# A hand-ordered attention kernel: short dummy matmuls in its head, V cast two pairs at a time, Newton's roots in PSUM, and new instruction orders

## The chip, the cores and the metric

The kernel runs on one core of a Trainium2 chip. A core has five engines with a queue each: TensorE (PE in the profile; PEld is its loading of weights), VectorE (DVE), ScalarE (ACT), GpSimd (POOL) and SyncE (SP), which here only issues DMAs. Each works through its own list in order and waits on semaphores for the others. The metric is the device time of one execution in microseconds (us), lower is better. Three runs of the kernel before gave 189.88, 192.01 and 192.94 us; their median is 192.01.

## The reference

```python
batch, heads, seq, dim = 8, 12, 512, 64        # Q, K, V float32, tau = 0.1
Q_norm = Q / (np.linalg.norm(Q, axis=-1, keepdims=True) + 1e-10)
K_norm = K / (np.linalg.norm(K, axis=-1, keepdims=True) + 1e-10)
scores = np.einsum('bhqd,bhkd->bhqk', Q_norm, K_norm) / tau
weights = np.exp(scores - np.max(scores, axis=-1, keepdims=True))
weights = weights / (np.sum(weights, axis=-1, keepdims=True) + 1e-10)
return np.einsum('bhqk,bhkd->bhqd', weights, V).astype(np.float32)
```

It is attention with cosine similarity: the rows of Q and K are brought to length one, and so the scores lie between -10 and 10 and their exponentials need no maximum taken off.

## The kernel before, in words

The 96 heads are worked in 48 pairs (`s` in the code), each head of a pair with 512 rows of 64 numbers, laid out as 128 partitions by 4 rows. For a pair:

- SP loads Q, K (`LD`, L312 and L315) and V (`LV`, L318) into rings of 17 and 9 buffers.
- POOL squares Q and K (`SQ`, L341; L335 for the first pairs, a part of which ACT does, L333).
- The sums of squares (`RED`) come in two ways: DVE adds up 64 columns itself (L369), or PE first adds eight groups of columns with an identity matrix (`SSQ`, L358) and DVE adds the remaining eight (L365). In the first four pairs both Q and K go over PE.
- The inverse roots (`NEW`) are made by DVE for a whole group of one to four pairs: a first guess by integer arithmetic on the bits (L403), then two Newton steps of three instructions each (L394, L395, L399). For pairs 0 and 1 ACT makes them by logarithm and exponential (L256 and L258, L383 and L386).
- Q and K are scaled by them and cast to bf16 (`SCL`, L427; Q on DVE, K mostly on POOL). PE transposes them (`TR`, L433) into PSUM, DVE copies them out (`EVA`, L441).
- PE makes the scores in four chunks of 128 keys by two heads by 512 queries (`SCO`, L532) in two alternating PSUM buffers of two banks each. ACT takes the exponential of a chunk in one instruction of 128x1024 (`EXP`, L548). One chunk in all, chunk 3 of pair 43 (the table `OFF`), goes through a polynomial on DVE and POOL instead (`poly`).
- POOL casts V to bf16, beside a column of ones (`VC`, L553). PE multiplies (`PV`, L565), DVE divides by the column sums (`RCP` L576, `NRM` L578), and SP stores the pair (`ST`, L582).

Pair 0 goes through a head of its own (`head0`): it is loaded, squared, scaled, transposed and scored by single heads (L521), and its exponentials are 8 of 128x512 (L524), with K's inverse norm as their scale. Before it PE runs eight matmuls on zeros (`warm`, L191) and one more dummy (L194). A dummy writes into the second of the two PSUM banks that PV uses. The last pair's end is cut into pieces (`last`).

Nothing sets the order at run time. `ORDER` holds, for each engine, the list of all its operations by number, with negative numbers for dummy matmuls of so many columns; the waits are worked out from the needs that `P.add` is given. An engine that waits holds up everything behind it.

## Time and profile before

| | |
|---|---|
| Runs | 189.88, 192.01, 192.94 us (median 192.01) |
| Span of the profiled execution | 190.9 us |
| Its own time outside the profile | not given; the span is all that the page has |
| ACT busy | 182.7 us, 96% of the span |
| PE, DVE, POOL busy | 175.9, 170.2, 161.8 us |
| Large exponentials | 186, 171.3 us busy, 0.6 us idle before them |
| First large exponential starts | 15.18 us |
| Last instruction of ACT ends | 188.8 us |

The page gives busy times, a picture of the span in 40 slices, the chain of work that ended last, and groups of instructions with the idle time before them. In rows of groups "x186 | 171.3, 1113 | 0.6" means 186 instructions, 171.3 us busy together, 1113 ns each, and 0.6 us in which their engine had been idle just before them. Instructions of one engine overlap a little at their ends, so the mean is longer than the distance from one to the next. A row of the chain has its start, its length, and the engine, tile and line.

### The profile page before, as it was taken

Reading aid. Unit: us, or ns where it says so; the run is one execution under the profiler, and the core shown is the slowest. Engines: PE = TensorE matmul, PEld = TensorE weight load, DVE = VectorE, ACT = ScalarE, POOL = GpSimd, SP = SyncE. Lnnn points to the kernel's source line nnn. Section 1 sums busy time; section 2 is a strip of 40 time slices with the busy share of each in tenths; the row PEclk is TensorE's granted clock in tenths of the full one; section 3 lists DMA queues with packets and bytes.
Section 4 is the critical chain, followed back from the end, with each engine's and each line's share of the span. In section 5 each row is a group of like instructions: output and inputs, shape, how many; then the busy total and the mean of one; then the engine's idle time right before and its main releaser. Section 6 shows DMA issues by size and latency. Waiting matters only on the chain.

```text
span 190.9 us, 6650 instructions
## 1 busy us (share of the span) xinstructions
PE 175.9 (92%) x2705; PEld 109.4 (57%) x2705; DVE 170.2 (89%) x552; ACT 182.7 (96%) x215; POOL 161.8 (85%) x150
## 2 busy tenths in 40 slices
PE   7699699999999999999999999999999899897973
PEld 2355266666656666666566666556656565464642
DVE  2668999999999999999997998999999999988642
ACT  5678999999999999999999999999999999999994
POOL 5397898999999999999999999999999994793000
PEclk9958999999999999999999999999999999999998
DMA  5999999997999599999979999999950414000565
GB/s 162 344 348 349 350 348 372 365 297 250 268 351 337 169 260 320 357 366 369 380 277 272 351 377 364 354 379 384 365 194 5 165 58 165 3 0 3 193 197 165
DMA packets 52446, 50.76 MB, mean 266 GB/s; under 512 B 3136, under 2 KB 52416, under 8 KB 52416
## 3 DMA queue, kind: packets, MB, share of 16 engines
q1 hardware_dynamic: 51984, 50.02, 79.7%
q8 instruction: 21, 0.34, 0.8%
q10 hardware_dynamic: 432, 0.33, 0.5%
q14 instruction: 9, 0.07, 0.1%
HBM read 37.75 MB, written 12.58 MB: 264 GB/s over the span
## 4 chain that ended last, share of the span: by engine, by line
ACT 89%; PE 4%; DMA 3%; DVE 1%; issue 0%; SPq 0%
ACT et L548 88%; DMA qk<-in_Q_dram 3%; PE ops L358 2%; PE scps L521 1%; PE tps L433 1%; DVE qn L427 1%; PE scps L532 0%; SPq L312 0%; ACT et L543 0%; ACT sq L333 0%; ACT ob L608 0%; PE tps L270 0%; DVE qn L261 0%; DVE ob L612 0%; PE ops L593 0%
## 5 line engine op out<-in xcount | busy, mean ns | idle before, releaser
L548 ACT ACTIVATE et<-scps 128x1024 bf16<-128x1024 f32 x186 | 171.3, 1113 | 0.6 <-PE scps L532 0.4
L341 POOL TENSOR_TENSOR sq<-qk 128x1024 bf16<-128x1024 f32 x44 | 83.1, 1896 | 0.1
L532 PE MATMUL scps<-qt 64*128 64x512 bf16 x374 | 73.3, 387 | 6.3 <-ACT et L548 3.3
L565 PE MATMUL ops<-vb,et 128*128 128x65 bf16 x1504 | 72.8, 195 | 1.7 <-DVE ob L578 1.0
L565 PEld LDWEIGHTS ops<-vb,et 128*128 128x128 bf16 x1504 | 55.3, 98 | 30.9 <-issue 18.3
L427 POOL TENSOR_TENSOR qn<-qk,rk 128x512 bf16<-128x512 f32 x38 | 39.5, 1045 | 5.9 <-PE scps L532 3.7
L578 DVE TENSOR_TENSOR ob<-ops,rd 128x256 f32<-128x256 f32 x94 | 38.8, 418 | 0.7
L427 DVE TENSOR_TENSOR qn<-qk,nps 128x512 bf16<-128x512 f32 x56 | 37.2, 677 | 0.7 <-ACT nps L386 0.6
L433 PE MATMUL tps<-ident,qn 128*128 128x128 bf16 x376 | 34.3, 222 | 0.9 <-POOL qn L427 0.3
L441 DVE COPY qt<-tps 128x1024 bf16<-128x1024 bf16 x47 | 32.1, 682 | 0.4 <-PE tps L433 0.4
L532 PEld LDWEIGHTS scps<-qt 64*128 64x128 bf16 x374 | 18.2, 92 | 23.5 <-ACT et L548 9.6
L369 DVE TENSOR_REDUCE nps<-sq 128x8 f32<-128x512 bf16 x46 | 30.8, 682 | 0.8 <-POOL sq L341 0.7
L553 POOL TENSOR_SCALAR vb<-vf 128x512 bf16<-128x512 f32 x48 | 29.7, 630 | 0.1
L433 PEld LDWEIGHTS tps<-ident,qn 128*128 128x128 bf16 x376 | 21.9, 99 | 12.0 <-issue 5.4
L576 DVE RECIPROCAL rd<-ops 128x4 f32<-128x4 f32 x94 | 16.1, 174 | 6.6 <-PE ops L565 5.9
L358 PE MATMUL ops<-sq,ident 128*128 128x64 bf16 x384 | 20.0, 199 | 0.1
L358 PEld LDWEIGHTS ops<-sq,ident 128*128 128x128 bf16 x384 | 15.2, 101 | 4.3 <-issue 2.5
L365 DVE TENSOR_REDUCE nps<-ops 128x8 f32<-128x64 f32 x46 | 10.0, 218 | 0.9 <-PE ops L358 0.7
L394 DVE TENSOR_TENSOR nps<-nps,ys 128x32 f32<-128x32 f32 (+2 forms) x34 | 7.0, 207 | 0.4
L395 DVE SCALAR_TENSOR_TENSOR nps<-nps,ys 128x32 f32<-128x32 f32 (+2 forms) x34 | 7.0, 206 | 0.4
L335 POOL TENSOR_TENSOR sq<-qk 128x512 bf16<-128x512 f32 (+1 forms) x5 | 4.7, 956 | 3.2 <-DMA qk<-in_K_dram 2.8
L524 ACT ACTIVATE et<-scps,xs 128x512 bf16<-128x512 f32 x8 | 4.9, 682 | 0.3 <-PE scps L521 0.3
(66 smaller groups left out, 57.8 us busy)
## 6 DMA issues: line engine op xcount, KB each, us to landing
vf<-in_V_dram SPq DMA_DIRECT2D x48, 256.0 KB, 6.6
qk<-in_Q_dram SPq DMA_DIRECT2D x47, 256.0 KB, 5.5
qk<-in_K_dram SPq DMA_DIRECT2D x47, 256.0 KB, 6.3
out_dram<-ob SPq DMA_DIRECT2D x47, 256.0 KB, 5.7
qk<-in_Q_dram SPq DMA_DIRECT2D x2, 128.0 KB, 2.7
qk<-in_K_dram ACTq DMA_DIRECT2D x2, 128.0 KB, 2.8
out_dram<-ob SPq DMA_DIRECT2D x1, 128.0 KB, 1.7
out_dram<-ob SPq DMA_DIRECT2D x1, 64.0 KB, 1.6
```

Source lines behind the costliest of these rows:

```text
L341: lambda e: e.tensor_tensor(out=sqf, in0=data, in1=data, op=ALU.mult))
L358: last = e.matmul(out=o_ps[bank][:, 320:384], lhsT=ident[:, :], rhs=sq[iqs][:, 8 * w : 8 * w + 8, 8 * k : 8 * k + 8], start=(k == 0), stop ...
L369: lambda e, w=w, dst=dst: e.tensor_reduce(out=dst, in_=sq[iqs][:, 8 * w : 8 * w + 8, :], axis=AX.X, op=ALU.add))
L427: lambda e, w=w, r=r: e.tensor_tensor(out=qn[iqn][:, w].rearrange("p t h d -> p h t d"), in0=qk[iq][:, w].rearrange("p h (t d) -> p h t d" ...
L433: last = e.transpose(t_ps[:, w, t, :], qn[iqn][:, w, t].rearrange("p h d -> p (h d)"), ident[:, :])
L441: lambda e: e.tensor_copy(out=qt[iqt][:, :, :, :].rearrange("p w t x -> p (w t x)"), in_=t_ps[:, :, :, :].rearrange("p w t x -> p (w t x)")))
L532: last = e.matmul(out=sc_ps[:, 2 * b + h, :], lhsT=qt[iqt][64 * h : 64 * h + 64, 1, c, :], rhs=qt[iqt][64 * h : 64 * h + 64, 0, :, :], sta ...
L548: lambda e, c=c, b=b: e.activation(out=et[iet][:, c, :, :], in_=sc_ps[:, 2 * b : 2 * b + 2, :], func=ACT.Exp, scale=math.log(2.0) / UNIT i ...
L553: lambda e: e.tensor_scalar(out=vb[:, iq, :, :, 0:DIM].rearrange("p c h d -> p h c d"), in0=vf[iv][:, :, :].rearrange("p h (c d) -> p h c ...
L565: last = e.matmul(out=o_ps[h][:, 65 * t : 65 * t + 65], lhsT=et[iet][:, c, h, 128 * t : 128 * t + 128], rhs=vb[:, iq, c, h, :], start=(c = ...
L576: lambda e, h=h, grid=grid: e.reciprocal(out=rd[io][:, h, :], in_=grid[:, :, DIM]))
L578: lambda e, h=h, grid=grid: e.tensor_tensor(out=ob[io][:, h], in0=grid[:, :, 0:DIM], in1=rd[io][:, h, :].unsqueeze(2).to_broadcast([128, N ...
```

## The change

- **Dummies.** The eight warm-up matmuls stay. The one dummy of 256 columns gives way to fourteen of 128 columns, spread over PE's list from the first transposes to the second part of pair 0's PV.
- **Sums in one bank.** The norm sums that PE makes for pairs 1 to 3 all go through the first PV bank; before, Q's went through the first and K's through the second. Each waits for DVE's reduction of the one before.
- **V.** Its f32 buffers become one tensor with a ring of 8 pairs (9 before), its bf16 buffers get a ring of their own of 16 (17, shared with Q and K, before) and another layout. From pair 4 on POOL casts two pairs in one instruction, which waits for both loads.
- **Newton.** The sums and iterates lie in SBUF (`xs`, `ts`), the roots in PSUM (`n_ps`); before, sums and iterates were in PSUM and the guesses in SBUF. Where DVE scales some K of a group, its last step makes Q's and K's roots at once, in place of two steps; where it scales all of them, the step for POOL's copy goes too. Counted over all groups, 144 steps become 135.
- **Polynomial.** It is written in another form: three POOL steps in place of four, two DVE steps as before. A scale that was an instruction of its own (`UNIT`) moves into the constants of Newton's last step, and the exponentials of the four pairs of that group get another scale.
- **Orders.** All five lists of `ORDER` are new.

```diff
-        session[s, w] = (w, due_red(s), before[w])
-        before[w] = [("RED", s, w)]
+        session[s, w] = (0, due_red(s), before[0])
+        before[0] = [("RED", s, w)]
...
+    def news(g):
+        if g in NORM_ON_ACT:
+            return [7] if direct_r(g) else [6, 7]
+        return [*range(6), *([6] if on_pool(g) else []), 7]
+
+    def on_pool(g):
+        return [i for i in range(first[g], first[g] + sizes[g]) if i not in K_ON_DVE]
...
-        xg = n_ps[:, g % R_X, 0 : 2 * m]
-        tg = n_ps[:, g % R_X, 64 : 64 + 2 * m]
-        yg = ys[g % R_X][:, 0 : 2 * m]
+        xg, tg, yg = xs[g % R_X][:, 0 : 2 * m], ts[g % R_X][:, 0 : 2 * m], n_ps[:, g % R_X, 0 : 2 * m]
...
-                yx, yyx, up(yg, 0, 2 * m), yx, yyx, up(rq_g, 0, m), up(rk_g, m, 2 * m)]
-            if on_dve:
-                steps.append(up(tg[:, m : 2 * m], m, 2 * m))
+                1: yx, 2: yyx(1.0), 3: up(yg, 0, 2 * m, 1.0), 4: yx, 5: yyx(c_g), 6: up(rk_g, m, 2 * m, c_g),
+                7: up(yg, 0, 2 * m, c_g) if on_dve else up(rq_g, 0, m, c_g)}
...
-        steps = [("pool", "yt", mul(z, z, z)), ("pool", "ys", add(w, z, a1)), ("pool", "yt", mul(w, w, w))]
-        if form == "A":
-            steps += [("pool", "ys", add(w, w, a2)), ("dve", "yd", fused(e_, z, a3, w)), ("dve", "ym", mul(e_, e_, p2))]
+        steps = [
+            ("pool", "yt", mul(z, z, z)),
+            ("pool", "ys", lambda e: e.tensor_scalar(out=w, in0=z, scalar1=a1, scalar2=a2, op0=ALU.add, op1=ALU.mult)),
+            ("pool", "yt", mul(w, w, z)),
+            ("dve", "yd", lambda e: e.scalar_tensor_tensor(out=e_, in0=w, scalar=a3, in1=z, op0=ALU.add, op1=ALU.mult)),
+            ("dve", "ym", mul(e_, e_, p2))]
...
+        n = len(cast_with[s])
+        if s == cast_with[s][0]:
+            P.add(("VC", s), "pool", f"vc{n}" if n > 1 else "vc", T0 + 3.0 - slack(s, M_VC),
+                  [("LV", i) for i in cast_with[s]] + [key("PV", i - R_VB, h, NT - 1) for i in cast_with[s] for h in range(2)] + ["vone"],
+                  lambda e: e.tensor_scalar(
+                      out=vb[:, ivb : ivb + n, :, :, 0:DIM].rearrange("p n h c d -> p (n h c) d"),
+                      in0=vf[:, iv : iv + n].rearrange("p n h (c d) -> p (n h c) d", c=NT),
+                      scalar1=1.0, scalar2=1.0, op0=ALU.mult, op1=ALU.mult))
...
-RINGS = (17, 9, 6, 4, 4, 5, 8, 3)
+RINGS = (17, 8, 16, 6, 4, 4, 5, 8, 3)
+MOST = 64
+CAST_ALONE = 4
+CAST_TOGETHER = 2
...
     "pe": (
-        "6 24 22 -256 38 52 40 36 76 78 44 48 54 42 114 46 116 83 85 50 159 87 161 89 57 58 59 63 91 60 128 130 93 "
+        "6 24 22 -128 38 44 52 -128 36 48 -128 40 -128 76 78 -128 54 42 -128 -128 -128 -128 114 46 116 -128 -128 "
```

Three places in the orders. In them `qn` are scaled rows, `qt` transposed ones, `scps` scores, `ops` the two PV banks, `tps` the bank of transposes, `ys` or `ya` logarithms, `xs` or `xa` sums and inverse norms. PE, from the end of the warm-up to the norm sums of pair 1, before:

```order
L272 MATMUL ops<-ident,qn 64x128 x4
L272 MATMUL tps<-ident,qn 64x128 x4
L194 MATMUL ops<-warm_in,ident 128x256
L270 MATMUL ops<-ident,qn 128x128 x4
L521 MATMUL scps<-qt 128x512 x2
L270 MATMUL tps<-ident,qn 128x128 x4
L358 MATMUL ops<-sq,ident 128x64 x16
L521 MATMUL scps<-qt 128x512 x4
```

and now:

```order
L208 MATMUL ops<-warm_in,ident 128x128
L285 MATMUL ops<-ident,qn 128x128 x4
L540 MATMUL scps<-qt 128x512 x2
L208 MATMUL ops<-warm_in,ident 128x128
L285 MATMUL tps<-ident,qn 128x128 x4
L540 MATMUL scps<-qt 128x512
L208 MATMUL ops<-warm_in,ident 128x128
L540 MATMUL scps<-qt 128x512
L208 MATMUL ops<-warm_in,ident 128x128
L385 MATMUL ops<-sq,ident 128x64 x16
```

All four score matmuls of pair 0's first head now stand ahead of pair 1's norm sums, where two stood, and dummies stand between them.

ACT, in the head, from the first inverse norm to the sixth-last exponential of pair 0, before:

```order
L258 ACTIVATE scps<-ys 128x4
L256 ACTIVATE ys<-xs,eps 128x4 x2
L258 ACTIVATE xs<-ys 128x4
L333 ACTIVATE sq<-qk 128x512
L258 ACTIVATE nps<-ys 128x4
L256 ACTIVATE ys<-xs,eps 128x4
L333 ACTIVATE sq<-qk 128x256
L524 ACTIVATE et<-scps,xs 128x512 x2
L383 ACTIVATE ys<-xs,eps 128x16
L258 ACTIVATE xs<-ys 128x4
L386 ACTIVATE nps<-ys 128x16
```

and now:

```order
L273 ACTIVATE scps<-ya 128x4
L254 ACTIVATE qn<-qk 128x4x64
L271 ACTIVATE ya<-xa,eps 128x4 x2
L273 ACTIVATE nps<-ya 128x4
L273 ACTIVATE xa<-ya 128x4
L360 ACTIVATE sq<-qk 128x512
L273 ACTIVATE xa<-ya 128x4
L360 ACTIVATE sq<-qk 128x256
L543 ACTIVATE et<-scps,xa 128x512 x2
L408 ACTIVATE ya<-xa,eps 128x16
L412 ACTIVATE nps<-ya 128x16
```

The inverse norm of Q's second head (to `nps`) moved from behind the squares of pair 1 to ahead of them, and an inverse norm of K (to `xa`) from between pair 1's logarithm and its root to ahead of the exponentials.

SP, the first loads of whole pairs, with buffer numbers, before:

```order
L315 DMA qk2<-in_K_dram 128x2x256
L318 DMA vf0<-in_V_dram 128x2x256
L315 DMA qk3<-in_Q_dram 128x2x256
L315 DMA qk3<-in_K_dram 128x2x256
L318 DMA vf1<-in_V_dram 128x2x256
L315 DMA qk4<-in_Q_dram 128x2x256
```

and now:

```order
L342 DMA qk2<-in_K_dram 128x2x256
L342 DMA qk3<-in_Q_dram 128x2x256
L342 DMA qk3<-in_K_dram 128x2x256
L342 DMA qk4<-in_Q_dram 128x2x256
L345 DMA vf<-in_V_dram 128x2x256
L342 DMA qk4<-in_K_dram 128x2x256
```

The first load of V moved behind three more loads of Q and K. Further on SP's list is out of the order of pairs: the Q of pair 12 is loaded ahead of the Q of pair 9, for example.

More of the change, by code (lines that the diff above doesn't have):

```diff
@@ L298, in last_direct @@
         d = [g for g in NORM_ON_ACT if g > 0]
-        return [("NEW", max(d), 7 if direct_r(max(d)) else 6)] if d and group[s] not in NORM_ON_ACT and s < 12 else []
+        return []
     def pair(s):
@@ L382, in pair @@
+        if s == first[g] and acts:
+            at, lo = NORM_ON_ACT[g], ya[g][:, 0 : 2 * m]
             P.add(("LOG", g), "act", "ln", at, reds + ["eps"],
[L383 to L388 removed]
@@ new lines, in pair @@
+            for k in news(g):
+                needs = [done] if k else reds + [("SCL", i, w) for i in past for w in range(2) if w == 0 or i in K_ON_DVE]
+                if k == 0 and g == R_X:
+                    needs += [("NRMS", 0, w, h) for w in range(2) for h in range(2)] + [("SCL", 0, 0, h) for h in range(2)]
+                if k == 6:
+                    needs += [("SCL", i, 1) for i in past if i not in K_ON_DVE]
+                done = ("NEW", g, k)
+                P.add(done, "dve", "new7" if k == 7 and on_dve else "new", TF - 4.9 - slack(s, M_NEW) + (M_STEP * (k - 7) if s > 8 else 0.23 * k), needs, steps[k])
@@ L453, in last_step @@
     def last_step(s, c):
-        return {"A": 5, "B": 4, "C": 5, "P": 6}[OFF[s, c][1]]
+        return 4
     def exps(s, c):
```

168 lines of the change are left out of this document (83 added, 85 removed), and 160 rows, old and new, of the table ORDER.

## The prediction

> **What bounds the kernel now.** I read the page first: the span, the busy line of each engine, the rows of slices and the chain that ended last.
>
> ```profile
> span 190.9 us, 6650 instructions
> PE 175.9 (92%) x2705; PEld 109.4 (57%) x2705; DVE 170.2 (89%) x552; ACT 182.7 (96%) x215; POOL 161.8 (85%) x150
> ...
> ACT  5678999999999999999999999999999999999994
> ...
> PEclk9958999999999999999999999999999999999998
> ...
> ACT 89%; PE 4%; DMA 3%; DVE 1%; issue 0%; SPq 0%
> ```
>
> ACT is 89% of the chain, and its row falls below nine only in the first four slices and in the last one. The row of the granted TensorE clock has a dip in the same place, slices three and four. Next I read the groups of instructions, then the chain in order of time.
>
> ```profile
> L548 ACT ACTIVATE et<-scps 128x1024 bf16<-128x1024 f32 x186 | 171.3, 1113 | 0.6 <-PE scps L532 0.4
> L524 ACT ACTIVATE et<-scps,xs 128x512 bf16<-128x512 f32 x8 | 4.9, 682 | 0.3 <-PE scps L521 0.3
> ```
>
> ```profile
> 15.13 0.53 PE ops L358 x8
> ...
> 15.69 0.23 DVE nps L365
> ...
> 16.14 1.20 DVE qn L427 x2
> ...
> 17.39 0.40 PE tps L433 x4
> 17.79 0.34 PE scps L532 x2
> ...
> 18.15 116.56 ACT et L548 x127
> ...
> 186.46 0.68 ACT et L543
> ```
>
> The 186 large exponentials wait 0.6 us in all. From 18.15 us on the chain is ACT without a break: 127 of them in 116.56 us is 0.918 us each, and 186 x 0.918 = 170.7 us is a floor that this change does not touch, since the same one chunk of scores (pair 43, chunk 3) goes to the polynomial before and after. After the last exponential begins (186.46) come 190.9 - 186.46 = 4.4 us of tail, whose work also stays. What is left to win lies ahead of 18.15 us, and there the chain runs through PE and DVE, not ACT.
>
> ```profile
> 5.00:6.60 1.60, 1.38 (x14) 0.90 (x13) 1.39 (x4) 0.38 (x3) 0.21 (x1) 1.00 1.00 318
> 6.60:8.50 1.90, 0.62 (x3) 0.14 (x4) 0.47 (x2) 1.23 (x5) 0.46 (x1) 1.00 1.05 360
> 8.50:10.00 1.50, 1.41 (x22) 1.11 (x24) 1.03 (x3) 1.14 (x2) 1.36 (x3) 0.56 1.10 366
> 10.00:12.00 2.00, 2.00 (x14) 0.66 (x13) 1.33 (x3) 1.67 (x6) 1.79 (x2) 0.50 1.10 348
> ...
> 15.20:18.20 3.00, 2.95 (x47) 1.88 (x46) 2.61 (x11) 2.88 (x4) 2.93 (x2) 0.95 1.13 353
> ```
>
> The columns of this view by stages are the stage, its length, the busy time of PE, weight loads, DVE, ACT and POOL, then the granted clock, the DMA share and GB/s. In 6.60:8.50 PE works 0.62 of 1.90 us, and right after it the clock halves: a mean of 0.56 in 1.50 us puts the drop at about 8.7, and 0.95 in 3.00 us puts the return at about 15.5. For 6.8 us PE is busy nearly throughout, at half rate, and the chain runs through it. This is the head's loss.
>
> **ACT in the head.**
>
> ```profile
> 7.28 0.63 ACT L333 ACTIVATE sq<-qk 128x512 bf16<-128x512 f32 x1 [1.90 <-DMA qk<-in_Q_dram]
> ...
> 8.40 1.24 ACT L524 ACTIVATE et<-scps,xs 128x512 bf16<-128x512 f32 x2
> 10.34 0.31 ACT L383 ACTIVATE ys<-xs,eps 128x16 f32<-128x16 f32 x1 [0.69 <-DVE xs L365]
> 10.55 0.19 ACT L258 ACTIVATE xs<-ys 128x4 f32<-128x4 f32 x1
> ...
> 10.80 2.98 ACT L524 ACTIVATE et<-scps,xs 128x512 bf16<-128x512 f32 x5
> 14.09 0.69 ACT L524 ACTIVATE et<-scps,xs 128x512 bf16<-128x512 f32 x1 [0.31 <-PE scps L521]
> 15.18 14.99 ACT L548 ACTIVATE et<-scps 128x1024 bf16<-128x1024 f32 x16 [0.40 <-PE scps L532]
> ```
>
> ACT waits 0.69 + 0.31 + 0.40 = 1.40 us after 8.40, each time for something that came through the slow PE. The first large exponential starts at 15.18, the fourth at 18.15.
>
> **The change, part by part.**
>
> *Head.* The squares of pair 1 need its loads, whose places in the queue stay, so ACT reaches the first exponential at 8.40 as before. But the inverse norm of Q's second head now stands ahead of those squares on ACT, not behind them. It is made while ACT waited 1.90 us, so PE gets the second head's transposes and all four score matmuls of the first head before 8.7, where it used to get two of these; four of the fourteen dummies lie there too. The norm sums of pair 1 then find PE free.
>
> ```profile
> L335 POOL TENSOR_TENSOR sq<-qk 128x256 bf16<-128x256 f32 x1 | 0.6, 613 | 2.8 <-DMA qk<-in_K_dram 2.8
> ```
>
> ```profile
> 19.57 0.41 PE L358 MATMUL ops<-sq,ident 128*128 128x64 bf16 x8
> ```
>
> ```profile
> 11.04 2.04 POOL L335 TENSOR_TENSOR sq<-qk 128x512 bf16<-128x512 f32 x2 [0.21 <-DMA qk<-in_Q_dram]
> ```
>
> Pair 1's Q lands by 7.28 and pair 3's Q, five loads on, by 11.04: 0.75 a load, so pair 1's K lands at 8.03, and POOL's half of its squares ends at 8.03 + 0.61 = 8.64. One group of sum matmuls takes 0.41 at full rate (0.53 at half, above), its reduction 0.23, and since both groups now use one bank the second waits for the first's reduction: some 0.6 more than the square's end if the groups don't overlap. The sums are there at about 8.64 + 0.6 + 0.41 + 0.23 = 9.9. ACT's logarithm starts at 9.9 and not 10.34, and without the 0.19 instruction that moved away the exponentials resume at about 10.3 and not 10.80. Six of them at (2.98 - 0.68) / 4 = 0.575 us, unbroken, end at 13.75. So the first large one could start 1.43 us earlier.
>
> Can it be fed? The rows are from the groups of instructions and from DVE's timeline.
>
> ```profile
> L532 PE MATMUL scps<-qt 64*128 64x512 bf16 x374 | 73.3, 387 | 6.3 <-ACT et L548 3.3 <-DVE qt L441 1.2 <-DVE qn L427 0.3
> L433 PE MATMUL tps<-ident,qn 128*128 128x128 bf16 x376 | 34.3, 222 | 0.9 <-POOL qn L427 0.3 <-DVE qt L441 0.2
> ```
>
> ```profile
> 17.25 0.18 DVE L394 TENSOR_TENSOR nps<-nps,ys 128x16 f32<-128x16 f32 x1
> 17.46 0.18 DVE L395 SCALAR_TENSOR_TENSOR nps<-nps,ys 128x16 f32<-128x16 f32 x1
> ...
> 17.83 0.69 DVE L441 COPY qt<-tps 128x1024 bf16<-128x1024 bf16 x1
> ```
>
>  The scaling and transposes of pair 1 follow the roots: 10.35 + 0.6, the reduction of pair 2's sums that DVE now takes between the two scalings, 0.6 again, a 0.4 us transpose, two Newton steps, the 0.69 copy: 13.2. Then the scores, 0.39 (their full-rate mean), which gives 13.65: in time.
>
> Next DVE limits. From that copy to the end of pair 2's scalings it has a dozen small steps at about 0.21 (17.46 - 17.25, start to start) and two scalings at 0.6, with one wait for pair 3's sum: I get 16.15 for the second scaling, before 17.34. Behind it on PE stand 0.40 of transposes and 0.34 of scores, so the fourth large exponential starts at 16.9 and not 18.15, 1.25 earlier. Pair 2's copy then ends at about 17.6, its first exponential starts at 18.0 and not 18.15 + 0.92 = 19.07, 1.07 earlier; pair 3's copy at about 21.7 gives back another 0.1. From there ACT is fed. I take **1.1 us** off the start of the unbroken stretch. The bounds are 0 (the clock drops again, next part) and 1.43 (only ACT's own list counts).
>
> *Dummies.* A 128-column matmul with its weights costs 34.3 / 376 = 0.09 us in the transposes' row; 14 cost 1.3 us. All stand where PE next waits for DVE, POOL or ACT, so I cost them at nothing with a full clock; at half clock the ten after 8.7, some 0.2 each, would add up to 2 us to PE's own work, against the transposes and scores that left the stretch.
>
> On the clock the Trainium skill, "TensorE: Matmul & The Clock Gate", says (Why this matters for your kernels) that only PE gaps above about 3 us bring the half rate back; by that the drop here should not have happened, the dummies would be worth nothing and the time would be rival A's. The stages above disagree: with PE busy 0.62 of 1.90 us it fell, so I give that rule no chance of its own. The same page says the windows of 3413 ns run free of the kernel's start; no row here can show that, and by it some executions of either kernel would drop and some not.
>
> *Newton, sums, polynomial.* Counted in the code, Newton's steps fall from 144 to 135 and one rescaling goes: 10 x about 0.2 = 2 us of DVE's 170.2. Roots lie in PSUM and the iterates in SBUF, the reverse of before; the rows show both kinds of output.
>
> ```profile
> L399 DVE SCALAR_TENSOR_TENSOR nps<-nps,ys 128x16 f32<-128x16 f32 x11 | 1.8, 175 | 0.0
> ...
> L399 DVE SCALAR_TENSOR_TENSOR rk<-nps,ys 128x16 f32<-128x16 f32 x8 | 1.3, 168 | 0.1
> ```
>
> PSUM output costs 175 ns, SBUF 168: a few ns either way, 0.5 us at most over all. DVE is not on the chain after 18.15, so this moves nothing; it is cover for ACT's earlier start.
>
> *V cast by two pairs.* The cast, and the POOL operation of twice its size that is nearest to it:
>
> ```profile
> L553 POOL TENSOR_SCALAR vb<-vf 128x512 bf16<-128x512 f32 x48 | 29.7, 630 | 0.1
> ...
> L488 POOL TENSOR_SCALAR xw<-xz 128x1024 f32<-128x1024 f32 x1 | 1.0, 1049 | 0.1
> ```
>
> One cast takes 630 ns for 512 elements, the operation on 1024 takes 1049. 22 joint casts cost 1.05 to 1.26 each instead of 1.26: 0 to 4.6 us less POOL work; I take 4.6, the same element count. The polynomial also drops one such 1.05 us step. POOL is off the chain: worth nothing at the end, but each joint cast needs the later of two V loads, and POOL is in order.
>
> *Sum.* Span 190.9 - 1.1 = 189.8. The page gives the profiled execution no time but its span; the runs' median, 192.01, is 1.1 above it, and I carry that over: **190.9 us**.
>
> **Rivals.**
>
> *A, the clock still falls.* In the 3.4 us ahead of the drop, half of the 6.8, PE was busy about 1.9 us (1.38 less 0.3 of its first stage, 0.62, and 0.2), a share of 0.56. Two more score matmuls, four more transposes and three more dummies, about 0.6 us, make it 0.73; in 15.20:18.20, at whose end the clock is full, it is 0.98. The threshold may lie on either side of 0.73: that speaks for this rival, and against it that PE's idle share is what sets these stages apart. Then PE at half rate sets the head again, about 0.3 us won from the order, 0.3 lost to dummies: 192.0. The Trainium skill's clock page (Part 4) adds that transposes do not count as busy; by it the gain in counted work would be smaller, which favours this rival.
>
> *B, slower: POOL stands at a cast.* V's first load moves behind three more Q and K loads on SP, and from there SP's list is out of sequence: loads wait behind loads and stores of other pairs. POOL's casts stand ahead of squares and scalings that DVE and PE wait for, and PE's values matmuls wait ahead of the next scores. POOL's longest wait before, from the list of waits:
>
> ```profile
> POOL qn L427 <- PE scps L532: 3.7, 1, 3.7
> ```
>
> At 0.75 a load V's first, now seven behind pair 1's Q, lands at 7.28 + 7 x 0.75 = 12.5, and POOL reaches its cast at about 12.9 (8.64 and four squares of about 1.04, half of 2.04). The margin is 0.4 us; the mechanism decides once POOL's stands, here and at the 22 joint casts, pass their cover by 1.1 us together. One stand like the longest that POOL had gives 3.7 - 1.1 = 2.6 us, 194.6.
>
> Against this rival: POOL has less work, and squares run ahead of their use by six buffers.
>
> *C, DVE's saving pays.* If the 0.6 us that large exponentials waited and the head's full 1.43 all go, 192.0 - 2.0 = 190.0; still within 2%.
>
> **How the numbers follow.** My forecast 0.5, A 0.22, B 0.2 (half of it past 2%, which needs 1.1 + 3.8 = 4.9 us of stands), C 0.08. The likeliest gives 190.9. The three runs of before reach from 189.88 to 192.94, so a median can be off by about a us: the low end is C less 0.8, 189.2; the high end takes in A, and B's one stand nearly, 194.2. A change of 2%, 3.8 us, is about what a measurement of this kernel can tell from none. Faster needs under 188.2, below every case here, left to scatter: 0.04. Slower is half of B: 0.1. Within 2%: 0.86.
>
> **What would show it.** Right: the granted clock at 1.00 from 5 us on, the first large exponential at 13.6 to 14.1, the chain on ACT alone from about 17, at most 1 us idle before the large exponentials, DVE near 168 busy and POOL near 156. Rival A: a clock of 0.5 between 8 and 16 again. Rival B: POOL waiting for V's loads, and PE's values matmuls or scores behind it, with several us before the large exponentials. Wrong altogether if the large exponentials wait for DVE's copies in the steady stretch.

## The result, and the profile after

The changed kernel takes 193.72 us, the median of 14 runs (192.71 to 199.29); the kernel before took 190.81 beside it, the median of 14 (189.88 to 192.94). The ratio is 1.014, with a 95% interval from 1.0109 to 1.0172: slower by 1.4%, where I had forecast 1.1 us less. The profile taken with the result fell into one of its slow executions (196.99 us), so the rows of after here come from a further profiled execution of the same kernel, 195.1 us with a span of 193.2. First its page: span, busy times, the slices of ACT and of the clock, the chain, and the large exponentials.

```profile
span 193.2 us, 6678 instructions
PE 176.4 (91%) x2718; PEld 111.9 (58%) x2718; DVE 169.9 (88%) x542; ACT 182.9 (95%) x215; POOL 157.6 (82%) x127
...
ACT  4789999999999999999997899999999999999992
...
PEclk9999999999999999999998799999999999999999
...
ACT 69%; PE 17%; DVE 9%; DMA 1%; issue 1%; POOL 1%
...
L567 ACT ACTIVATE et<-scps 128x1024 bf16<-128x1024 f32 x186 | 171.6, 1107 | 2.2 <-PE scps L551 2.0
```

The dip of the clock in the head is gone in this execution, as forecast. It is not gone for good: in the other profile of the same kernel PE was at half rate in the head, by the lengths of its matmuls (eight for a norm sum took 0.63 us, here 0.40), and the first large exponential started at 17.46 us. Here ACT and the clock now have a dip in slices 22 and 23, ACT's share of the chain fell from 89% to 69%, and the large exponentials waited 2.2 us and not 0.6. There is a new stall near 105 us. In the other profile it is small: the large exponentials waited 0.7 us there.

The other half of the answer is in a second profile of the kernel *before*, unaltered (190.62 us, span 188.7). Its page and ACT's timeline:

```profile
span 188.7 us, 6650 instructions
...
PEclk9999999999999999999999999999999999999999
```

```profile
9.06 0.31 ACT L383 ACTIVATE ys<-xs,eps 128x16 f32<-128x16 f32 x1
...
9.52 3.56 ACT L524 ACTIVATE et<-scps,xs 128x512 bf16<-128x512 f32 x6
12.94 9.50 ACT L548 ACTIVATE et<-scps 128x1024 bf16<-128x1024 f32 x10
```

Here the clock does not fall in the head, and the first large exponential starts at 12.94 us, not at 15.18. ACT's timeline after:

```profile
10.22 0.31 ACT L408 ACTIVATE ya<-xa,eps 128x16 f32<-128x16 f32 x1 [0.77 <-DVE xa L392]
...
10.68 3.56 ACT L543 ACTIVATE et<-scps,xa 128x512 bf16<-128x512 f32 x6
14.11 8.37 ACT L567 ACTIVATE et<-scps 128x1024 bf16<-128x1024 f32 x9
```

Three spans make up an execution: to the first large exponential, from there to the end of the last one, and the tail. Before (second profile) they are 12.94, 171.43 and 4.33 us; after, 14.11, 173.79 and 5.30. So 1.2 us were lost in the head, 2.4 in the stretch and 1.0 in the tail of these two executions.

### The profile page after: what moved, and what is told of

Its sections match the earlier page's. It is cut to its first block, busy times and chain, and to the rows that moved or that the text cites. A ratio compares the mean times of both kernels' runs of the same rounds, so it can differ in the third digit from the quotient of the medians.

```text
span 195.3 us, 6678 instructions
## 1 busy us (share of the span) xinstructions
PE 179.7 (92%) x2718; PEld 113.2 (58%) x2718; DVE 170.4 (87%) x542; ACT 184.0 (94%) x215; POOL 157.5 (81%) x127
## 4 chain that ended last, share of the span: by engine, by line
ACT 55%; PE 23%; DVE 11%; DMA 5%; SPq 3%; issue 2%; POOL 1%; DVEq 0%
ACT et L567 54%; PE ops L587 7%; PE scps L551 6%; DMA out_dram<-ob 3%; PE tps L457 3%; DVE qn L451 2%; PE scps L540 2%; PE ops L385 2%; DVE qt L465 2%; DVE ob L604 2%; SPq L342 2%; SPq L608 2%; DMA qk<-in_Q_dram 1%; DVE xs L396 1%; PE ops L208 1%
## 5 line engine op out<-in xcount | busy, mean ns | idle before, releaser
L368 POOL TENSOR_TENSOR sq<-qk 128x1024 bf16<-128x1024 f32 x44 | 82.7, 1893 | 0.8 <-DMA qk<-in_Q_dram 0.5
L587 PE MATMUL ops<-vb,et 128*128 128x65 bf16 x1504 | 76.2, 195 | 1.5 <-DVE ob L604 1.2
L587 PEld LDWEIGHTS ops<-vb,et 128*128 128x128 bf16 x1504 | 57.8, 98 | 29.5 <-issue 18.2
L451 POOL TENSOR_TENSOR qn<-qk,rk 128x512 bf16<-128x512 f32 x38 | 39.2, 1043 | 14.3 <-DVE rk L426 14.3
L396 DVE TENSOR_REDUCE xs<-sq 128x8 f32<-128x512 bf16 x46 | 30.6, 675 | 0.0
L575 POOL TENSOR_SCALAR vb<-vf 128x1024 bf16<-128x1024 f32 (+1 forms) x26 | 25.3, 981 | 0.8 <-DMA vf<-in_V_dram 0.8
L392 DVE TENSOR_REDUCE xs<-ops 128x8 f32<-128x64 f32 x46 | 9.7, 210 | 1.5 <-PE ops L385 1.3
L543 ACT ACTIVATE et<-scps,xa 128x512 bf16<-128x512 f32 x8 | 5.2, 683 | 2.6 <-PE scps L540 2.6
L419 DVE TENSOR_TENSOR ts<-xs,nps 128x32 f32<-128x32 f32 (+2 forms) x34 | 6.6, 194 | 0.6
L426 DVE SCALAR_TENSOR_TENSOR nps<-ts,nps 128x32 f32<-128x32 f32 (+3 forms) x34 | 6.6, 195 | 0.4
L422 DVE SCALAR_TENSOR_TENSOR ts<-ts,nps 128x32 f32<-128x32 f32 (+2 forms) x34 | 6.6, 194 | 0.5
```

What stands on the lines that cost most here:

```text
L368: lambda e: e.tensor_tensor(out=sqf, in0=data, in1=data, op=ALU.mult))
L396: lambda e, w=w, dst=dst: e.tensor_reduce(out=dst, in_=sq[iqs][:, 8 * w : 8 * w + 8, :], axis=AX.X, op=ALU.add))
L451: lambda e, w=w, r=r: e.tensor_tensor(out=qn[iqn][:, w].rearrange("p t h d -> p h t d"), in0=qk[iq][:, w].rearrange("p h (t d) -> p h t d" ...
L575: lambda e: e.tensor_scalar(out=vb[:, ivb : ivb + n, :, :, 0:DIM].rearrange("p n h c d -> p (n h c) d"), in0=vf[:, iv : iv + n].rearrange( ...
L587: last = e.matmul(out=o_ps[h][:, 65 * t : 65 * t + 65], lhsT=et[iet][:, c, h, 128 * t : 128 * t + 128], rhs=vb[:, ivb, h, c, :], start=(c ...
```

## The experiments

**First pair of theories: the order, or the operations.** CODE: one of the changed operations, buffers or waits costs, in any order. ORDER: the head's new order, or the new order behind it. Four kernels, all with the changed operations, cross the two orders of the head with the two behind it.

```diff
 # all with the operations of after; only the lists ORDER differ
 # head = all up to the first chunks of pair 1, with SP's first loads
-head of after,  rest of after     (the changed kernel again)
+head of before, rest of before    (one dummy of 256)
+head of after,  rest of before
+head of before, rest of after
```

> The changed kernel once more, nothing altered, for a second profiled execution. In its first one PE ran at half rate from 5.7 to 16.6 us by the lengths of its matmuls (a norm-sum group 0.53, a lone score matmul 0.54), although the column of the granted clock says 1.00 there; the first large exponential started at 17.46, the stretch from there to the last exponential took 172.9 us (171.3 before), the tail 4.9 (4.4 before). Theory HEAD (the clock's phase sets the loss): this time the first large exponential starts somewhere between 13.5 and 17.5, and the time moves with it one for one. Theory STRETCH (the new orders lose it behind the head): whatever the start, the stretch takes 172.5 to 173.2 again and the tail 4.8 to 5.0. Time 193 to 197, slower than before by 1 to 2%.

> The changed kernel's operations (joint casts, Newton with roots in PSUM, sums in one bank, the short polynomial), in the order of before, with its one dummy of 256 columns; a joint cast stands where the first of its two casts stood, and the last Newton steps of a group stand together. Theory CODE (an operation got dearer or a wait was added): as slow as the change, 193.5, 1.0% to 1.7% above before. Theory ORDER (head or stretch): like before, 190.8, within 0.4%.

> The changed kernel's operations; up to the copy of pair 2 and pair 1's exponentials in the new order, with the new dummies, behind that in the order of before. Theory HEAD: slow as the change, 193 to 194, with the first large exponential late in most executions. Theory STRETCH: 191 to 191.7, the stretch 171.0 to 171.6 and the tail 4.4; only what the head itself loses is left.

> The reverse: the head in the order of before with its one dummy, and the new order behind it. Theory HEAD: like before, 190.5 to 191.3. Theory STRETCH: 192.8 to 193.5, the stretch 172.5 to 173.2 and the tail 4.8 to 5.0, wherever the first large exponential starts.

Before took 190.2 us beside them (11 runs). Measured: the changed kernel 193.85 (ratio 1.0175, 1.0114 to 1.0237); the old order on all engines 195.41 (1.0241, 1.0197 to 1.0286); new head with the old rest 194.76 (1.0231, 1.0181 to 1.0281); old head with the new rest 193.7 (1.0167, 1.0117 to 1.0217). No order brings the time of before back, and with the changed operations the old one is no better, so the new order as a whole is not what costs. CODE is left, but with more than one place: the old order's stalls and the new order's lie elsewhere.

**The stall near 105 us.** ACT's waits there, what PE waited for, and POOL, in the changed kernel:

```profile
105.92 1.02 ACT L567 ACTIVATE et<-scps 128x1024 bf16<-128x1024 f32 x1 [1.35 <-PE scps L551]
107.24 1.02 ACT L567 ACTIVATE et<-scps 128x1024 bf16<-128x1024 f32 x1 [0.30 <-PE scps L551]
108.67 16.82 ACT L567 ACTIVATE et<-scps 128x1024 bf16<-128x1024 f32 x18 [0.41 <-PE scps L551]
```

```profile
104.50 0.62 PE L457 MATMUL tps<-ident,qn 128*128 128x128 bf16 x8 [1.32 <-POOL qn L451]
```

```profile
99.53 2.06 POOL L575 TENSOR_SCALAR vb<-vf 128x1024 bf16<-128x1024 f32 x2 [1.82 <-DMA vf<-in_V_dram]
```

Read backwards: ACT waits for scores, these for transposes, these for POOL's scaling, and POOL had stood 1.82 us for V's loads at a joint cast (the two casts of this row are those of pairs 24 with 25 and 28 with 29, by POOL's list). Why were the loads late? The waits of SP's queue, in the kernel before (second profile) and after (us in total, times, longest), and the stages 85 to 90 us of both (last three columns: granted clock, DMA share, GB/s):

```profile
SPq L318 <- POOL vb L553: 2.3, 5, 0.6
```

```profile
SPq L345 <- POOL vb L575: 21.6, 7, 5.3
```

```profile
85.00:90.00 5.00, 4.89 (x80) 3.11 (x76) 4.70 (x17) 5.00 (x6) 5.00 (x6) 1.00 1.10 374
```

```profile
85.00:90.00 5.00, 5.00 (x91) 3.47 (x90) 4.71 (x14) 5.00 (x7) 5.00 (x4) 1.00 0.40 122
...
105.00:110.00 5.00, 5.00 (x65) 3.11 (x62) 2.37 (x9) 3.38 (x4) 5.00 (x4) 0.66 1.09 381
```

SP stood 21.6 us at V's loads for POOL's casts (2.3 before). A buffer of V comes free only with a joint cast, and there are eight where there were nine. In 85 to 90 us the DMA's share falls to 0.40; the loads queued behind SP's stand all go out later, V's for pairs 24 and 25 among the last. At 105 to 110 us PE, which had stood 1.32 us, also has its clock at 0.66. RING was the name of this theory; three kernels should have taken the stand away, and a fourth run profiled the kernel before again.

```diff
-CAST_TOGETHER = 2
+CAST_TOGETHER = 1            # first: casts alone, the second half way to the next
-RINGS = (17, 8, 16, 6, 4, 4, 5, 8, 3)
+RINGS = (17, 10, 14, 6, 4, 4, 5, 8, 3)   # second: ten buffers for V
-"sp": the list of after
+"sp": the list of before     # third
```

> The changed kernel in its own order, with V cast pair by pair again (630 ns for 512 elements, twice, where the joint cast takes 1048; the first cast where the joint one stood, the second half way to the next). Theory RING: the joint cast frees V's eight buffers two at a time and needs both loads; SP stands 21.6 us at V's loads for POOL's casts (0.8 before), the DMA's idle and then everything comes late near 103 us. By it SP's stand at V's loads falls under 8 us, POOL's waits for V's loads fall under 1 us, the stalls of ACT near 103 us go, and the time is 191.5 to 192.5 although POOL is busy 4.6 us longer. Theory CODE (the Newton steps with roots in PSUM, or the norm sums in one bank, make a chain through PE and DVE longer): 193 to 195 as before the edit, with the stalls at other places.

> The changed kernel in its own order with joint casts, and ten buffers for V's loads where it has eight (two fewer for the casts' results: 14 for 16). RING: SP's stand at V's loads falls under 10 us, and the time to 191.5 to 192.5. CODE: 193 to 195. If SP's stand falls and the time stays, neither the ring nor the casts set the time, and the order of SP's list itself, or CODE, is left.

> The changed kernel in its own order on PE, ACT, DVE and POOL, with the list of SP taken from the kernel before: loads in sequence, V's first load ahead of pair 3, stores where they stood. RING in its wider form (the new list of loads and stores is what stands): SP's stands at V's loads are short, and the time 191.5 to 192.5. RING in its narrow form (joint casts need both loads): POOL waits for V's loads by 2 to 3 us as with the old order on all engines, and the time stays at 193 to 195. CODE: 193 to 195 with no wait for V to speak of.

> The kernel before, unaltered, once more with a profile. If the profile that the forecast was made from was a typical execution, its first large exponential starts at 15.0 to 15.4 and the clock halves between 8 and 16 us by the lengths of matmuls. If that loss is an accident of that execution, the first large one starts at 12.6 to 13.4, the span is 188 to 189, and the stretch from there to the end of the last one about 171.5.

All three missed their forecasts: 200.06 us (ratio 1.0458, 1.0384 to 1.0532), 198.21 (1.0328, 1.0231 to 1.0424) and 206.27 (1.078, 1.0705 to 1.0855), beside 191.38 of before; the fourth is the second profile of before shown above. But none of the three took the stand away, and that is why they tell something: SP's longest single stand at V's loads was 7.0 us with casts alone (the later cast frees the buffer still later), 11.1 with ten buffers, and 14.3 with the list of before. With ten buffers one long stand was left, and DVE waited for stores:

```profile
SPq L345 <- POOL vb L575: 11.5, 2, 11.1
```

```profile
DVE ob L604 <- DMA out_dram<-ob: 4.8, 2, 4.0
```

The new list puts the loads of V for pairs 35 and 34 ahead of those for 30 to 33. With ten buffers pair 35's waits for the cast of pair 25, which POOL has late in its list; behind it stood the stores of pairs 16 to 20, and DVE's division waited for their buffers. So these two loads were moved behind the store of pair 17; in a second kernel the old head was added; a third run asked what the dummies are worth; and a fourth took the old order with casts alone, at the places that they had before.

```diff
 "sp":
-... LV24 LV35 LD40 LV34 LD38 ST16 ... LD42 ST17 LV31 ...
+... LV24 LD40 LD38 ST16 ... LD42 ST17 LV35 LV34 LV31 ...   # with ten buffers
 "pe": (third run, else as after)
-"6 24 22 -128 38 44 52 -128 36 48 -128 40 ...
+"6 24 22 38 44 52 36 48 40 ...
 # fourth run: the lists of before, and
-CAST_TOGETHER = 2
+CAST_TOGETHER = 1
```

> The changed kernel with ten buffers for V's loads, as in the run with more of them, and two of V's loads (pairs 35 and 34) moved behind the store of pair 17 in SP's list: in that run SP stood 11.1 us at the load of pair 35, whose buffer the late cast of pair 25 frees, with the stores of pairs 16 to 20 behind it; DVE waited 4.8 us for a store, and one stall of 7 us at 110 us was all that the large exponentials lost. Theory SP (one stand in SP's list sets the loss in the stretch; the rest of the changed kernel is no slower than before): the stall goes, the stretch is 170.5 to 171.5 (before 171.4), the first large one at 14.1, the time 190.5 to 191.5. Theory ORDER in its strict form (any move in the searched order costs): another stand appears and the time stays above 193.

> The same with the head's order of the kernel before. Theory SP, and the head's new order costs 1 us where the clock is full: the first large exponential at 13.1, the stretch 170.5 to 171.5, the time 189.5 to 190.5, at or a little below the kernel before. Strict ORDER: above 193.

> The changed kernel without its fourteen short dummies, all else as it is. If they hold the clock up in the head: matmuls at half rate between 8 and 16 us, the first large exponential at 15 to 16.5, the median 0.5 to 2 us above the changed kernel's 193.7. If they are worth nothing: the first large one at 13.8 to 14.2 and the same time. If they cost PE's time: 13.5 or earlier.

> The changed kernel's other operations (Newton with roots in PSUM, norm sums in one bank, the shorter polynomial) in the order of the kernel before, and V cast pair by pair at the places that it had there. Against the same with joint casts (195.4, ratio 1.024) only the casts differ. Theory ORDER (an order fits only the operations, buffers and durations that it was searched for; the casts are what the old order does not fit): the stretch of large exponentials is 171.3 to 172.0 as before, no waits for V's loads, ratio 0.998 to 1.006. Theory CODE: stretch 173 or more, ratio 1.015 or more.

Moving the two loads: 191.95 us (ratio 1.01, 1.0033 to 1.0167), 1.9 less than the changed kernel. Its three runs without a profile took 191.79 to 192.08, below every one of the 18 runs of the changed kernel (from 192.34); the profiled one took 193.97. Its stand at V's loads and what is left of the stall:

```profile
SPq L345 <- POOL vb L575: 2.4, 1, 2.4
```

```profile
113.14 12.22 ACT L567 ACTIVATE et<-scps 128x1024 bf16<-128x1024 f32 x13 [0.78 <-PE scps L551]
```

21.6 us of stand became 2.4, and 2.06 us of ACT's waits became 0.78. So SP's stand at V's loads costs the changed kernel time, and the place is where POOL's joint casts meet the new list; how much it costs is not settled. The medians say 1.9 us, but the two intervals overlap. The stretch in the profile is 172.66 us, 1.1 less than 173.79 and not the 170.5 to 171.5 that I had expected (the time was to be 190.5 to 191.5). With the old head the same edit took only 0.4 us off, from 193.7 to 193.31 (1.0143, 1.0093 to 1.0193), a miss; the clock is at 0.62 and 0.52 there from 13 to 17 us. Nor does a stand of one length cost the same everywhere: in the old head with the new rest SP stood 19.4 us and the large exponentials waited 1.0 us, where the changed kernel had 21.6 and 2.2.

Without dummies: 194.15 us (1.0164, 1.0096 to 1.0232), no difference that can be measured. The granted clock of the whole execution was 0.982 to 0.991 in three of its four runs, and 0.997 to 1.000 in all four of the run with dummies and the moved loads; over the 18 runs of the changed kernel it was 0.961 to 1.000. Two stages of PE without dummies (busy, granted clock, DMA share, GB/s):

```profile
9.00:11.00 2.00, 1.27 (x18) 1.00 1.10 355
11.00:13.00 2.00, 1.96 (x18) 0.64 1.10 348
```

So the dummies help to hold the clock up in the head, but they do not ensure it. Of seven profiled executions with all fourteen, five were at full rate there; in two (the first profile of the changed kernel, and the kernel with casts alone in the new order) PE was at half rate by the lengths of its matmuls. Both profiled executions with the new head and no dummies (this one and one further down) were at half rate in a part of it. What it is worth is too little to see in the time.

**What costs in the old order.** Casts alone there took 196.35 us (1.0226, 1.0168 to 1.0283), no better than joint ones (195.41): neither ORDER nor the casts. Two kernels then put back, one after the other, the buffers of before and the two banks of the early norm sums; another gave the kernel before the one bank alone; and one more swapped Newton's places.

```diff
 # old order, casts alone, and
-RINGS = (17, 8, 16, 6, 4, 4, 5, 8, 3)
+RINGS = (17, 9, 17, 6, 4, 4, 5, 8, 3)
 # and, in the second and fourth kernel
-        session[s, w] = (0, due_red(s), before[0])
+        session[s, w] = (w, due_red(s), before[w])
 # fourth kernel: xs and ts in PSUM, and
-        yg = n_ps[:, g % R_X, 0 : 2 * m]
+        yg = yb[g % R_X][:, 0 : 2 * m]        # SBUF
 # third kernel: the kernel before with
-        session[s, w] = (w, due_red(s), before[w])
+        session[s, w] = (0, due_red(s), before[0])
```

> As the run with casts alone in the old order, and with the buffers of the kernel before as well: nine for V's loads and seventeen for their casts (eight and sixteen there, where SP stood 9.8 us at V's loads). What then differs from the kernel before is Newton with roots in PSUM, the norm sums of the first pairs in one bank, and the shorter polynomial. Theory BUFFERS: SP's stand at V's loads falls under 3 us, the stretch is 171.3 to 172.2, and 1 to 3 us of the 4.4 that were lost come back: 191.5 to 193.5. Theory NEWTON: the time stays above 194.

> The same, with the norm sums of pairs 1 to 3 alternating between two banks as in the kernel before. Left of the change are Newton and the polynomial. If the one bank makes PE wait for DVE's reductions in the head (0.64 and 0.55 us in the old order): the first large exponential at 12.8 to 13.2, the clock full as in the kernel before, 190.0 to 191.0, ratio 0.998 to 1.004. If Newton costs: ratio 1.01 or more.

> The kernel before with one thing of the change: the norm sums of pairs 1 to 3 in one bank. Theory BANK (the second sum has to wait until DVE has reduced the first, so ACT's logarithm and all behind it is late, and PE stands): the first large exponential at 13.6 to 14.3 where the kernel before alone had 12.94, and 191.5 to 193.5, ratio 1.006 to 1.016. If the bank costs only together with the other edits: 190 to 191.

> As the run with two banks, and the places of Newton's data swapped back: iterates in PSUM, roots in SBUF, as in the kernel before. Left of the change are the order in which Newton's results are made and the polynomial. Theory PLACE (roots in PSUM cost): 190 to 191, ratio below 1.004. If the place is worth nothing, as forecast (0.5 us at most over all of DVE): 192 to 193, ratio 1.006 to 1.012.

The buffers: 195.88 us (1.0275, 1.0191 to 1.036) beside 191.67 of before, so nothing is won. The two banks: 192.76 (1.0083, 1.0039 to 1.0128), 3.1 us less. A part of that is the clock: at granted clocks of 0.984 to 0.988 the kernel with one bank took 194.61 and 194.74 us, the one with two 192.95 to 193.82. The bank alone in the kernel before: one run at a granted clock of 0.997 took 191.43 us, 1.05 more than the median of before beside it, 190.38; one run gives no interval. Three runs at 0.962 to 0.972 took 194.79 to 195.78. PE in that kernel, in one of these three: the row of its sums of pair 2's K, and three stages.

```profile
11.76 0.58 PE L358 MATMUL ops<-sq,ident 128*128 128x64 bf16 x8 [0.56 <-DVE nps L365]
```

```profile
7.00:9.00 2.00, 0.86 (x15) 1.00 1.08 377
9.00:11.00 2.00, 1.39 (x21) 1.00 1.10 356
11.00:13.00 2.00, 1.44 (x17) 0.55 1.10 348
```

With one bank PE stands for DVE's reductions. A fall of the clock went with it more often than with two: of 45 runs of the kernel before that were taken beside the experiments only one had a granted clock of 0.972 or less, of these four runs three. That the one stand brought on the fall is not shown. A mean of 0.55 in 11 to 13 us puts the fall at about 11.2, which is where the stand shown (11.20 to 11.76) begins and not where it ends. What the bank costs without a fall can be counted from the start of pair 1's first sum to ACT's logarithm: two executions with two banks took 1.05 and 0.93 us (8.01 to 9.06 in the second profile of before), three with the old head and one bank 1.60 to 1.72. So it is some 0.6 us. The starts of the large exponentials agree: with the head at full rate the first one starts at 12.94 and 12.40 with the old head and two banks, at 13.12, 13.52 and 13.82 with the old head and one, and at 14.11 to 14.19 in five executions with the new head and one.

The swap took 249.15 us (1.3045, 1.296 to 1.313) and missed both theories, for a reason of my own making: in the kernel before the roots that DVE scales by were in PSUM too, and only the guesses were in SBUF. So it says nothing on Newton's place, which stays open, but shows something else (last section). What remains at 192.76 us over the kernel before, 0.8%, is not settled between Newton, the polynomial, the layout of V and the clock: five of these ten runs had 0.984 to 0.988, and the profile has a fall at 21 us (last section).

**Both losses undone in the new order**, without dummies (they write into the second bank), with the new head and the old.

```diff
 # ten buffers for V, LV35 and LV34 moved, no dummies (old head: one of 256), and
-        session[s, w] = (0, due_red(s), before[0])
+        session[s, w] = (w, due_red(s), before[w])
```

> The changed kernel in its own order with ten buffers for V's loads and the two loads moved (191.95 us with dummies and one bank), here with the norm sums of pairs 1 to 3 in two banks, and without the dummies, since they write into one of those banks. BANK: the first large exponential at 13.2 to 13.8 (14.1 with one bank); whether the time gains depends on the clock without dummies: 190.5 to 191.5 at full, 192 to 193.5 if it halves.

> Ten buffers, the two loads moved, two banks, the head's order of the kernel before, and the new order behind it. If the theories hold together (stand in SP's list gone, bank undone, the old head a little sooner): the first large one at 12.3 to 12.9, the stretch 171.0 to 172.0, the time 189 to 190.5, ratio 0.992 to 1.0. If order costs wherever it is not the one searched: 192 or more.

Measured: 194.63 us (191.16 to 195.35) and 193.62 (190.91 to 196.04) beside 190.38. The two runs of the second with a granted clock of 0.995 and 1.000 give a ratio of 1.004, 0.9972 to 1.0108; of the first one run took 191.16 and three 194.23 to 195.35, and there is no interval. Their profiles are of executions in which PE was at half rate until about 17 us, by the lengths of its matmuls. In the first, the stretch was 171.76 us, 0.3 more than before's 171.43, without any stall of ACT behind its start. So with the stand undone the new order can be nearly as fast behind the head; it was not each time, as the 172.66 us further up, with the same order there, show. No version here beats the kernel before.

## Why the prediction was wrong

The range, 189.2 to 194.2, held 193.72, and the chances put most on a change under 2%. The direction was wrong, by these steps.

*"What is left to win lies ahead of 18.15 us"*: this is the step that failed. I took the half-rate head, 8.7 to 15.5 us, for a property of the kernel. It was one of that execution: the second profile has 12.94 for 15.18 us. In the sum the same error stands as "the runs' median, 192.01, is 1.1 above" the span: in the second profile the time is 190.62 - 188.7 = 1.9 above the span, and in the 45 runs of the kernel before beside the experiments 1.75 to 2.08. So the span of 190.9 belonged to the slowest of the three runs, 192.94, and not to the median. Of these 45 runs 28 had a granted clock of 0.995 or more and took 189.76 to 191.38 us; 17 had 0.991 or less (the forecast's profile 0.979) and took 191.29 to 195.16. In most executions there was no such loss for the change to remove.

*The head, step by step*, ended near its numbers. Sums there at 9.9: measured 9.96 + 0.23 = 10.19. Logarithm at 9.9: 10.22. Exponentials resumed at 10.3: 10.68. First large one at 13.75: 14.11, a third of a us off, at the edge of the 13.6 to 14.1 named as the sign of being right. But that is in part luck. ACT's last square of pair 1 and the two sums in the changed kernel, and PE's sums in the second profile of before and in the run without dummies:

```profile
7.38 0.40 ACT L360 ACTIVATE sq<-qk 128x256 bf16<-128x256 f32 x1
```

```profile
8.72 0.40 PE L385 MATMUL ops<-sq,ident 128*128 128x64 bf16 x8
9.53 0.39 PE L385 MATMUL ops<-sq,ident 128*128 128x64 bf16 x8 [0.41 <-ACT et L543]
```

```profile
8.01 0.75 PE L358 MATMUL ops<-sq,ident 128*128 128x64 bf16 x16 [0.15 <-ACT sq L333]
```

```profile
8.35 0.41 PE L385 MATMUL ops<-sq,ident 128*128 128x64 bf16 x8
```

I had the loads hold the squares back to 8.64; they ended at 7.78. *"The norm sums of pair 1 then find PE free"* failed by as much: the sums began at 8.72, since scores, transposes and dummies of the new list stood ahead of them. The two errors offset each other. (The row puts the second sum's wait down to ACT; by the needs in the code it is for DVE's reduction of the first sum, which ended at 9.16 + 0.23 = 9.39.) With PE's old list and two banks, in the second profile of before, the sums began at 8.01, as soon as the squares were there, and the logarithm started at 9.06. Of the 1.16 us by which it is later now, 0.7 is the later start and some 0.45 the one bank, which I had priced ("some 0.6 more"). Against the true 12.94 the first large exponential lost 1.2 us.

*The dummies at nothing with a full clock*: not quite. Without them pair 1's sums began at 8.35, and the logarithm at 9.85 and not 10.22: some 0.4 us on the path, in one execution. *Rival A*: the clock did fall in some executions with the dummies, and in both profiled ones without them; the times did not decide it.

*"From there ACT is fed"*: this failed too. I took the 186 large exponentials for a floor that the change does not touch. Their stretch was 171.46 and 171.43 us in the two profiles of before, and 173.79 after. Only rival B had a price for that.

*Newton "moves nothing"*: not shown either way. Ten steps went (552 to 542 instructions), but DVE's busy time fell from 170.0 to 169.9 us, not by 2.

*Joint casts at 1.05*: right, and POOL went from 161.8 to 157.6 us:

```profile
L575 POOL TENSOR_SCALAR vb<-vf 128x1024 bf16<-128x1024 f32 x22 | 22.9, 1048 | 2.7 <-DMA vf<-in_V_dram 2.7
```

The same row has the cost: 2.7 us of waits for V's loads, 0.1 before. *Rival B*, chance 0.2, was the right mechanism in its second form ("loads wait behind loads and stores of other pairs"; POOL stands at a cast). I placed it at the first cast or at a single later stand, priced 3.7 - 1.1 = 2.6 us; it is at the casts near 99 us, and undoing it gave 0.4 to 1.9. What I missed is where it comes from: not the order of loads alone, but SP standing for a buffer that a joint cast frees late.

*"4.4 us of tail, whose work also stays"*: 5.5 by the same count in the execution shown (193.2 - 187.70). Most of the difference is the landing of the last store, 2.4 us for 1.7 (rows below), which the change does not touch.

The sum with these corrections: 190.8 + 1.2 (head) + 1.9 (stand, by the medians) = 193.9, for 193.72 measured. It comes out only with the highest price of the stand; with 0.4 some 1.3 us would have no cause. That part stays open.

## What to carry to other kernels

One profile is one execution: before a loss in it is priced as something to win, compare its span with the spread of the runs, or look at a second profile. Work that is put ahead of a step on the critical path is not free because the engine will wait later. When transfers are freed by a merged instruction, count the engine that issues them as waiting for the later of its parts, and look at what is queued behind. Sharing a bank between two steps cost its wait here, some 0.6 us; more executions also lost PE's clock, by which of its waits is open.

## What the runs showed of the hardware

*A fall of the clock without a long gap.* In the kernel before with one bank the clock was 0.55 in 11 to 13 us. PE had been busy 0.86 and 1.39 us in the two stages of 2 us ahead of it, and its longest wait in them was this one:

```profile
7.58 0.40 PE L270 MATMUL tps<-ident,qn 128*128 128x128 bf16 x4 [0.72 <-DVE qn L261]
```

The Trainium skill, "TensorE: Matmul & The Clock Gate" (Why this matters for your kernels), warns of gaps above about 3 us; here the clock fell with none above 0.72 us. The share of work is not a sharp bound either: 1.27 of 2.00 us was followed by a fall without dummies (9 to 11 us, above), while the kernel before had the same 1.27 in 19 to 21 us of its second profile, and no fall in the next stage. The kernel with two banks in the old order comes last (busy time of PE, weight loads, DVE, ACT and POOL, granted clock, DMA share, GB/s):

```profile
19.00:21.00 2.00, 1.27 (x10) 0.33 (x7) 1.93 (x12) 2.00 (x3) 2.00 (x3) 1.00 1.10 350
21.00:23.00 2.00, 1.48 (x19) 0.81 (x18) 2.00 (x5) 2.00 (x3) 2.00 (x3) 1.00 1.10 350
```

```profile
21.00:23.00 2.00, 2.00 (x18) 1.02 (x17) 1.97 (x5) 1.86 (x3) 2.00 (x3) 0.58 1.10 348
```

These two executions run the same matmuls there. The last one has a norm sum at 17.12 and scores at 18.45, 19.30, 19.96 and 20.88 us; the kernel before has them at 17.82, 19.15, 20.01, 20.66 and 21.58, each 0.70 or 0.71 later, with the same waits of 0.46, 0.27 and 0.53 us between the scores. In the one the clock falls at about 21.3 (0.58 as a mean of 2 us), in the other it stays. So some 4 us of the same work on PE can end with a fall or without one.

*Two operands in SBUF.* With the roots in SBUF, DVE's scaling took 1520 ns, and POOL's squares and casts slowed as well. First the kernel with swapped places, then the one with two banks, the same but for that:

```profile
L369 POOL TENSOR_TENSOR sq<-qk 128x1024 bf16<-128x1024 f32 x44 | 89.9, 2051 | 0.3 <-DVE nps L397 0.3
L452 DVE TENSOR_TENSOR qn<-qk,yb 128x512 bf16<-128x512 f32 x56 | 84.4, 1520 | 1.0 <-ACT yb L413 0.6
...
L576 POOL TENSOR_SCALAR vb<-vf 128x512 bf16<-128x512 f32 x48 | 38.1, 802 | 0.0
```

```profile
L368 POOL TENSOR_TENSOR sq<-qk 128x1024 bf16<-128x1024 f32 x44 | 83.0, 1893 | 0.2 <-DMA qk<-in_K_dram 0.2
...
L451 DVE TENSOR_TENSOR qn<-qk,nps 128x512 bf16<-128x512 f32 x56 | 37.1, 676 | 0.9 <-ACT nps L412 0.6
...
L575 POOL TENSOR_SCALAR vb<-vf 128x512 bf16<-128x512 f32 x48 | 29.3, 620 | 0.2 <-DMA vf<-in_V_dram 0.2
```

676 to 1520 ns, 1893 to 2051 and 620 to 802. The Trainium skill, "SBUF — State Buffer" (SBUF: two separate sides), says that a DVE operation with two SBUF inputs and a POOL operation that reads SBUF hold a shared pair of ports in turn, each for a whole instruction. The rows agree in that both engines lost. The PSUM operand is worth 844 ns an operation here; how much of it is waiting for POOL, and how much the operation's own time, no run shows.

*The last store lands in about 1.7 or in about 2.5 us.* The rows of DMA issues (KB each, median us to landing) of the kernel before, second profile, and of the changed kernel:

```profile
out_dram<-ob ACTq DMA_DIRECT2D x1, 64.0 KB, 1.7
```

```profile
out_dram<-ob ACTq DMA_DIRECT2D x1, 64.0 KB, 2.4
```

The changed kernel itself showed 1.8 in its other profile. Over all 20 profiles it was 1.6 to 1.8 in eleven, 2.4 or 2.5 in eight and 2.0 in one. What decides between them stayed open.
